# Attention of a hybrid encoder block: head pairs on 64-row tiles, first steps inside the last projection pair

## The chip, the core and the metric

The kernel is one program on one of the eight cores of a Trainium2 chip. A core has TensorE (PE, matrix products, with PEld for its weight loads), VectorE (DVE), ScalarE (ACT), GpSimd (POOL) and SyncE (SP, which only issues transfers); each works through its own queue in order. On-chip memory is SBUF (128 partitions) and PSUM (8 banks of 128 x 512 float32, where products land). The metric is device time in microseconds (us), smaller is better.

## The reference, cut to what matters

One layer on 1024 tokens of width 1024 in float32. After an RMS norm one projection gives all inputs of two branches:

```python
q, k, v, f_logit, g_b, g_c, hc, gate_conv, gate_attn = split(h @ w_in)
ya = g_b * causal_depthwise_conv(g_c * hc, conv_w)          # branch A, 512 channels
logf = log_sigmoid(f_logit + b_f); c = cumsum(logf)         # per head
logits = q @ k.T / 8 + c[t] - c[s], for s <= t only         # 8 heads of width 64
yb = softmax(logits) @ v                                    # branch B, 512 channels
merged = sigmoid(gate_conv) * (ya @ w_branch[0]) + sigmoid(gate_attn) * (yb @ w_branch[1])
x = x + rmsnorm(merged @ w_out)
x = x + rmsnorm(swiglu(rmsnorm(x)))                         # hidden width 2816
```

## The kernel before, in words

Products are made to nearly float32 accuracy from two reduced-precision parts. `split` rounds a matrix to `hi` on ACT (`copy`, L95) and takes the rest `lo` on DVE (`sub`, L89); `mm3` (L106 to L108) adds the three products hi hi, hi lo and lo hi. Large products are made by a Strassen-Winograd scheme (`strassen`), seven half-size products (`prod`) for a pair of 128-column weight blocks, whose sums are taken on DVE (`add`, L86).

The stages in order: norm and V projection; then `jobs`, 18 pairs of projections (4 of Q and K, 6 for the convolution, 8 pairs of the two gates), whose results go to DRAM (`qk_dram`, `ya_dram`, `sg_dram`, the last after a sigmoid); attention; branch B and the merge; the output product; the feed-forward part. Before the gate pairs are over, nothing of attention but the loads and splits of Q and K for the first pair can start: the PSUM pool `pss` opens only when the projections' pool `psm` of 8 banks closes.

Attention works through 64 units: 4 head pairs j, 8 blocks i of 128 query tokens (from the last to the first), 2 heads e. For a unit, `qk` (L708, L709) makes the logits of (i+1) x 128 keys. The 128 rows of the array hold a head's width of 64 twice: the stationary operand has q hi in one half and q lo in the other (`qk_stacks`), the moving operand k hi twice, then k lo twice, so two products per stretch of keys make all. Logits of over 512 keys take two banks (tile `sp`, tag S, two buffers of two banks). `softmax` adds the causal mask to the block of `cb` (c broadcast to all partitions) on POOL (L716), adds `cb` to the logits and takes the row minimum of the negated sum on DVE (L727), takes the exponential with its row sum on ACT (L731), and on DVE inverts the sum (L735) and scales the row (L736). `transp` turns the weights by 128 x 128 blocks on PE (L748) into the tile `tps` (two banks) and evacuates each four blocks on ACT (L95) or, one time in six, on DVE (L753). `pv_pair` (L764) multiplies with V, two heads on the two column halves of the array, and copies four query blocks at a time to `yb` on ACT.

Between units the products of branch A (`branch_a`, weights by `load_wa`, its product tile `pba`, one bank) fill PE; six of the eight row blocks of 128 output channels are made there, two (`RES`) after it. Each result is multiplied by its gate into `um` on DVE (L92). Then branch B splits its weights (`wbh`, `wbl`) and `yb` (`ybh`, `ybl`) and makes its products `pbb`.

The order of instructions on each engine is made when the program is built: a planner takes the instructions in program order, but lets one go ahead that its own estimate finds ready earlier. `tc.keep_in_program_order(ins)` pins an instruction behind the instruction traced before it on the same engine. Memory of a closed pool is used again, and the new tile waits for the readers of the tiles that it covers: `ybh` covers `yah`, which branch A reads to its end.

## Time and profile before

| what | us |
|---|---|
| median of 3 runs (1394.82 to 1399.31) | 1396.46 |
| the profiled execution | 1395.57 |
| its span, from the first to the last instruction | 1393.5 |
| TensorE busy | 1350.9 |
| VectorE, ScalarE, GpSimd busy | 967.1, 550.9, 141.1 |

The span is what the trace shows; the profiled execution has 2.1 us around it. The granted TensorE clock is 0.993 of full speed on average. In the rows below an instruction is named by its engine, its line, and `out<-in` by the program's tile names; a helper's line (L86, L89, L92, L95, L106 to L108) stands for all of its callers, so the tile names tell which one it is.

### The profile page before, as it was taken

The page shows a single profiled execution, that of the slowest core. Times are in us where ns is not written, and L with a number is a line of the kernel's source. Part 1 is how long each engine was busy: PE and PEld are TensorE (multiplying, and loading weights), DVE is VectorE, ACT ScalarE, POOL GpSimd, SP SyncE. Part 2 cuts the span into 40 slices and gives each one's busy share as a digit, 9 for nine tenths or more (in the row PEclk, how much of TensorE's full clock was granted, in tenths as well). Part 3 has the DMA queues.
Part 4 walks back from the last instruction along what each step waited for, and adds up shares of the span by engine and source line. Part 5 has one row for each costly group of instructions (what it writes and reads, how often), then busy time and mean ns, then how long its engine had stood idle before and what let it go on. Part 6 is the DMA issues. An engine that isn't in the chain of part 4 may idle for free.

```text
span 1393.5 us, 17697 instructions
## 1 busy us (share of the span) xinstructions
PE 1350.9 (97%) x6625; PEld 1108.1 (80%) x6625; DVE 967.1 (69%) x1557; ACT 550.9 (40%) x878; POOL 141.1 (10%) x260
## 2 busy tenths in 40 slices
PE   7999999999998999999999999999999999999987
PEld 6988888888886787778887788888888888888865
DVE  6883867655557787585669698776667766476695
ACT  6541222233347667433447332232232323444442
POOL 0001100011112222000001122100111101000000
PEclk9999999999999999999999999999999999999999
DMA  6332422333458432182234565222333326875471
GB/s 213 106 103 87 129 73 64 99 99 120 120 179 231 114 114 94 44 258 88 78 121 151 161 195 181 99 91 84 113 105 108 109 90 244 294 246 187 135 273 61
DMA packets 149670, 190.24 MB, mean 137 GB/s; under 512 B 9472, under 2 KB 102656, under 8 KB 149584
## 3 DMA queue, kind: packets, MB, share of 16 engines
q1 hardware_dynamic: 134272, 138.47, 32.8%
q0 software_dynamic: 15312, 50.64, 10.1%
q8 instruction: 52, 0.85, 0.3%
q14 instruction: 34, 0.28, 0.1%
HBM read 140.03 MB, written 49.05 MB: 136 GB/s over the span
## 4 chain that ended last, share of the span: by engine, by line
PE 88%; DVE 5%; DMA 3%; ACT 2%; issue 1%; SPq 0%; POOL 0%; DVEq 0%; ACTq 0%; POOLq 0%
PE b L106 18%; PE b L108 18%; PE b L107 18%; PE pd L106 4%; PE pd L108 4%; PE pd L107 4%; PE po L764 3%; PE tps L748 2%; PE pm L106 2%; PE pm L107 2%; PE pm L108 2%; PE pbb L107 1%; PE sp L708 1%; PE pbb L108 1%; DMA raw<-qk_dram 1%
## 5 line engine op out<-in xcount | busy, mean ns | idle before, releaser
L86 DVE TENSOR_TENSOR c<-c,b 128x512 f32<-128x512 f32 x200 | 136.5, 683 | 101.5 <-PE b L108 73.2
L95 ACT ACTIVATE hi<-raw 128x1024 fp32r<-128x1024 f32 x111 | 117.4, 1058 | 195.9 <-PE b L107 87.6
L89 DVE TENSOR_TENSOR lo<-raw,hi 128x1024 fp32r<-128x1024 f32 x104 | 127.1, 1222 | 97.5 <-PE b L108 69.0
L106 PE MATMUL b<-hth,hi 128*128 128x512 f32 x352 | 138.9, 395 | 0.0
L108 PE MATMUL b<-hth,lo 128*128 128x512 f32 x352 | 138.1, 392 | 0.0
L107 PE MATMUL b<-htl,hi 128*128 128x512 f32 x352 | 137.2, 390 | 0.0
L95 ACT ACTIVATE hi<-sx 128x1024 fp32r<-128x1024 f32 x40 | 42.5, 1061 | 221.3 <-PE b L107 195.7
L106 PE MATMUL pd<-hi 128*128 128x512 f32 x224 | 88.5, 395 | 5.1 <-DVE um L86 5.1
L108 PE MATMUL pd<-hi,lo 128*128 128x512 f32 x224 | 87.8, 393 | 0.0
L108 PEld LDWEIGHTS b<-hth,lo 128*128 128x128 f32 x352 | 66.1, 188 | 15.7
L107 PEld LDWEIGHTS b<-htl,hi 128*128 128x128 f32 x352 | 66.1, 188 | 14.7
L106 PEld LDWEIGHTS b<-hth,hi 128*128 128x128 f32 x352 | 66.2, 188 | 13.9
L89 DVE TENSOR_TENSOR lo<-sx,hi 128x1024 fp32r<-128x1024 f32 x40 | 49.0, 1225 | 34.4 <-PE b L108 30.8
L106 PE MATMUL b<-hah,hi 128*128 128x512 f32 x176 | 69.8, 399 | 1.5 <-ACT c L95 1.5
L89 DVE TENSOR_TENSOR sx<-raw 128x512 f32<-128x512 f32 x78 | 53.7, 688 | 22.5 <-DMA raw<-in_w_in_dram 12.2
L108 PE MATMUL b<-hah,lo 128*128 128x512 f32 x176 | 69.0, 393 | 0.0
L107 PE MATMUL b<-hal,hi 128*128 128x512 f32 x176 | 68.6, 390 | 0.0
L727 DVE CUSTOM_DVE_ANT_0 pt<-sp,cb 128x1024 f32<-128x1024 f32 (+7 forms) x64 | 48.1, 753 | 20.1 <-PE sp L709 9.8
L108 PE MATMUL b<-hT34h,lo 128*128 128x512 f32 x144 | 56.7, 394 | 0.0
L108 PE MATMUL b<-hT12h,lo 128*128 128x512 f32 x144 | 56.7, 394 | 0.0
L106 PE MATMUL b<-hT34h,hi 128*128 128x512 f32 x144 | 56.2, 390 | 0.4 <-DVE c L86 0.4
L731 ACT ACTIVATE pt<-pt,nm 128x1024 f32<-128x1024 f32 (+7 forms) x64 | 49.4, 772 | 17.9 <-DVE nm L727 15.9
(318 smaller groups left out, 3403.7 us busy)
## 6 DMA issues: line engine op xcount, KB each, us to landing
raw<-in_w_gate_up_dram SPq DMA_DIRECT2D x51, 512.0 KB, 4.0
raw<-in_w_in_dram SPq DMA_DIRECT2D x35, 512.0 KB, 4.2
graw<-in_w_down_dram SPq DMA_DIRECT2D x28, 512.0 KB, 5.0
a_dramS<-um POOLq DMA_DIRECT2D x44, 256.0 KB, 2.8
a_dramA<-um POOLq DMA_DIRECT2D x33, 256.0 KB, 2.9
xt<-in_x_dram SPq DMA_DIRECT2D x16, 512.0 KB, 4.2
raw<-qk_dram SPq DMA_DIRECT2D x32, 256.0 KB, 5.0
raw<-a_dramS SPq DMA_DIRECT2D x16, 512.0 KB, 3.7
```

The source lines that it names most:

```text
L86: nc.vector.tensor_tensor(o, a, b, op=ALU.add)
L89: nc.vector.tensor_tensor(o, a, b, op=ALU.subtract)
L95: nc.scalar.activation(o, a, AF.Copy)
L106: nc.tensor.matmul(ps, ah, bh, start=start, stop=False, **kw)
L107: nc.tensor.matmul(ps, ah, bl, start=False, stop=False, **kw)
L108: nc.tensor.matmul(ps, al, bh, start=False, stop=stop, **kw)
L708: nc.tensor.matmul(sp[:, b, :w], qs[:, qi], kh[:, k0:k1], start=True, stop=False)
L727: nc.vector.tensor_tensor_reduce(*args, 1.0, 3e38, op0=ALU.add, op1=ALU.min, accum_out=nm)
L731: nc.scalar.activation(pt[:, :n], pt[:, :n], AF.Exp, bias=nm, scale=-1.0, accum_out=rsum)
L748: nc.tensor.transpose(tps[:, k - k0, :], pt[:, k * P : (k + 1) * P], ident)
L764: nc.tensor.matmul(po[0][e * HD : (e + 1) * HD, i % 4, :], v[:, k, h * HD : (h + 1) * HD], pts[e][:, k, :], start=(k == 0), stop=(k == i),)
```

## The change

All of the following is one change.

- The last of the 18 projection pairs is written out by hand (`last_pair`) on two banks of its own (`pst`, tags ma and mb); the other pairs have 6 banks. Between its seven products stand the split of the first head pair's Q and K, the load of its V, and the logits and softmax of the first two steps. Its results are stored without the sigmoid, which is applied after they are loaded.
- A unit is now a step of both heads. Q and K of a pair are loaded once, with head 0 in partitions 0 to 63 and head 1 in 64 to 127, and the logits are products on 64 rows: q hi k hi, q hi k lo, q lo k hi, for head 0 and head 1 in turn, each head in its own bank.
- Row sums are kept; `inverse_rows` inverts them for a pair at once, turns them with a small transpose, writes them to DRAM and loads them broadcast, and `divide` scales `yb` with them instead of the weights.
- Order: every PE instruction of attention and of the last pair is pinned, and the splits of later operands on ACT and DVE. A step goes logits of t, softmax of t, first half of the transposes of t-1 (if it has more than four blocks), P.V of t-2, the other transposes; half a row block of branch A at the steps of `FILL`. The last pair takes query blocks 3 to 0 before 7 to 4, and its sums are inverted by halves.
- V is loaded per head pair by SP; `cb` has two buffers for even and two for odd pairs, `pt` likewise for steps; two of five evacuations of transposes go to DVE; gates are loaded by halves. In branch B `yb` is split ahead of the weights, the weights by halves.

```diff
-    def mm3(ps, a, b, start, stop, **kw):
+    def inorder(ins):
+        return tc.keep_in_program_order(ins)
+    def mm3(ps, a, b, start, stop, pin=lambda ins: ins, **kw):
...
-    psm, psm_close = pool("psm", 8, space=PSUM)
+    pst, pst_close = pool("pst", space=PSUM)
+    psm, psm_close = pool("psm", 6, space=PSUM)
...
+    def qk(j, i):
+        qh, ql, kh, kl = stacks[j]
...
+        for b, (k0, k1) in enumerate(parts):
+            for x, (q_, k_) in enumerate(((qh, kh), (qh, kl), (ql, kh))):
+                for e in range(2):
+                    r = slice(e * HD, (e + 1) * HD)
+                    out_ = sps[e][:, b] if wide else sps[0][:, e]
+                    inorder(
+                        nc.tensor.matmul(
+                            out_[:, : k1 - k0], q_[r, qi], k_[r, k0:k1],
+                            start=(x == 0), stop=(x == 2),
+                        )
+                    )
...
+    steps = [(j, i) for j in range(3) for i in reversed(range(ST))]
+    steps += [(3, i) for i in (3, 2, 1, 0, 7, 6, 5, 4)]
...
+    def last_pair(w):
...
+        pr(ma, "A11", B11, True)
+        copy(c21, ma)
+        inorder(nc.scalar.activation(warm, ones[:, 0:1], AF.Exp))
+        pr(mb, "A12", B21, True)
+        add(c11, c21, mb)
+        qk_split(0)
+        load_v(0)
+        pr(ma, "S2", T2, True)
+        add(c12, c21, ma)
+        pr(mb, "S1", T1, True)
+        add(c22, c21, mb)
+        step_qk(0)
+        pr(ma, "S3", T3, False)
+        add(c22, c22, ma)
+        step_softmax(0)
+        pr(mb, "S4", B22, False)
+        add(c12, c12, mb)
+        step_qk(1)
+        pr(ma, "A22", T4, False)
+        add(c21, c21, ma)
...
-        split(wh, wl, wr)
-        sg = tp_.tile([P, S], F32, tag="sg", name="sg", bufs=2)
-        nc.sync.dma_start(sg, sg_dram[d][0])
+        split(wh, wl, wr, inorder)
...
+    def inverse_rows(j, half=None):
...
+        nc.vector.reciprocal(ri, rs)
+        tr = pss.tile([P, 4, P], F32, tag="T", name="tr", bufs=2)[: 2 * w, 0, :]
+        inorder(nc.tensor.transpose(tr, ri.rearrange("p e i -> p (e i)"), ident))
...
+        nc.vector.tensor_copy(rT, tr)
+        for e in range(2):
+            nc.sync.dma_start(ri_dram[j][e][to]..., rT[e * w : (e + 1) * w, :])
...
+            nc.sync.dma_start(rb[e * HD : (e + 1) * HD, :], ri_dram[j][e][to].partition_broadcast(HD))
...
-        ri = st_tile("ri")
-        nc.vector.reciprocal(ri, rsum)
-        nc.vector.tensor_scalar(pt[:, :n], pt[:, :n], ri, None, op0=ALU.mult)
...
+    FILL = (7, 10, 13, 14, 15, 18, 21, 22, 23, 25, 26, 27)
+    step_softmax(1)
+    for t in range(1, NU + 4):
+        j, i = steps[t] if t < NU else (None, None)
+        if t > 2 and t < NU:
+            step_qk(t)
+            step_softmax(t)
+        if j is not None and j < 3 and i == 5:
+            cb_of(j + 1, 0)
+            cb_of(j + 1, 1)
+            qk_load(j + 1)
+            load_v(j + 1)
...
+            turn_ = transp(k_, pts.pop(t - 1), ptTs[t - 1])
+            if k_ > 3:
+                next(turn_)
+                next(turn_)
+            if t == 1:
+                step_qk(2)
+                step_softmax(2)
+        if 2 <= t < NU + 2:
+            pv_pair(*steps[t - 2], ptTs.pop(t - 2))
+        if t in FILL and steps[t - 1][1] < 4:
+            next(fill)
+        for _ in turn_:
+            pass
+        if t in FILL and steps[t - 1][1] > 3:
+            next(fill)
+        if j is not None and j < 3 and i == 4:
+            qk_split(j + 1)
+        if 2 <= t < 6:
+            load_ya(t - 2)
+        if t <= NU:
+            jj, ii = steps[t - 1]
+            if jj < 3 and ii == 0:
+                rbs[t + 3] = jj, inverse_rows(jj)
+            elif jj == 3 and ii % 4 == 0:
+                rbs[t + 3] = jj, inverse_rows(jj, ii // 4), ii // 4
+        if t in rbs:
+            divide(*rbs.pop(t))
...
     for d in range(KT - RES, KT):
         for _ in branch_a(d, load_wa(d), psm, "mm"):
             pass
...
-    for n in range(2):
-        ns = slice(n * NC, (n + 1) * NC)
+    for ns in (n1, n2):
         for k in range(4):
             split(ybh[:, k, ns], ybl[:, k, ns], yb[:, k, ns])
+        for k in range(4):
+            split(wbh[k][:, ns], wbl[k][:, ns], wbr[k][:, ns])
```

## The prediction

> **What bounds the kernel now.** I read the page first, then the busy time by stage, then the chain of waits and the timelines of the stages that lose time.

> ```profile
> span 1393.5 us, 17697 instructions
> PE 1350.9 (97%) x6625; PEld 1108.1 (80%) x6625; DVE 967.1 (69%) x1557; ACT 550.9 (40%) x878; POOL 141.1 (10%) x260
> ```

> TensorE is busy nearly throughout, so only idle or badly packed TensorE time can be won. The stages around attention (columns: time, then busy time and instructions of PE, weight loads, DVE, ACT and POOL, the granted clock, the DMA share, GB/s):

> ```profile
> 395.72:414.95 19.23, 19.23 (x86) 15.78 (x85) 9.89 (x11) 8.70 (x11) 2.30 (x5) 1.00 0.59 175
> 414.95:470.00 55.05, 46.74 (x324) 34.21 (x323) 41.50 (x90) 37.06 (x71) 14.51 (x23) 1.00 0.76 211
> 470.00:578.22 108.22, 106.61 (x879) 86.83 (x879) 83.73 (x218) 75.42 (x171) 26.35 (x45) 1.00 0.27 87
> 578.22:589.25 11.03, 11.03 (x49) 8.93 (x48) 2.06 (x3) 0.60 (x1) 0.00 (x0) 1.00 0.06 24
> 589.25:598.64 9.39, 6.71 (x21) 4.96 (x21) 9.19 (x12) 6.21 (x10) 0.00 (x0) 0.82 0.78 245
> ```

> The first row is the last projection pair. Attention runs from 414.95 to 578.22, 163.3 us; 578.22 to 589.25 is the two row blocks of branch A that are left over (48 products of 512 columns, 0.23 us each); 589.25 to 598.64 is the start of branch B, with PE idle and the clock at 0.82. In its first 55 us attention finishes 324 PE instructions, in the next 108 us 879. The chain of waits shows two long transfers in that first part, and the waits of PE what else holds it:

> ```profile
> 422.47 14.52 DMA raw<-qk_dram
> 460.13 7.79 DMA cb<-c_dram
> ```

> ```profile
> PE sp L708 <- DVE nm L727: 4.8, 3, 2.2
> ```

> Unit prices, from chain and timeline rows:

> ```profile
> 474.68 0.87 PE tps L748 x8
> 477.03 1.89 PE po L764 x30
> ```

> ```profile
> 476.10 0.93 PE L748 MATMUL tps<-ident,pt 128*128 128x128 f32 x7
> 476.96 1.96 PE L764 MATMUL po<-ptT,v 128*64 128x128 f32 x30
> 478.85 0.98 PE L748 MATMUL tps<-ident,pt 128*128 128x128 f32 x7
> 485.00 0.40 PE L108 MATMUL pba<-yah,s4l 128*128 128x512 f32 x1
> 485.23 0.40 PE L708 MATMUL sp<-lo,hi 128*128 128x512 f32 x1
> ```

> A transpose takes 0.87/8 = 0.109 us. A P.V product on a half-width tile takes 1.89/30 = 0.063 us; two of these, on the two column halves, take the 0.109 us of one full-width instruction, plus the entry and exit of the burst: after seven transposes (0.76 us) the next starts 0.86 later, so a change of tile shape costs 0.1 us. A 512-column logits product follows the one before by 0.23 us, which is 0.446 ns per column.

> The instruction counts of the whole stage, and below them those of the part after 470 for lines 708, 709, 748 and 764:

> ```profile
> L764 PE MATMUL po<-ptT,v 128*64 128x128 f32 x576 | 44.9, 280 | 2.2 <-DMA v<-v_dram 1.4 <-DVE ptT L753 0.4 <-ACT ptT L95 0.2
> L748 PE MATMUL tps<-ident,pt 128*128 128x128 f32 x288 | 43.1, 276 | 2.4 <-ACT ptT L95 1.6 <-DVE pt L736 0.5 <-ACT pt L731 0.2
> L736 DVE TENSOR_SCALAR pt<-pt,ri 128x1024 f32<-128x1024 f32 (+7 forms) x64 | 35.9, 561 | 1.2
> L735 DVE RECIPROCAL ri<-rsum 128x1 f32<-128x1 f32 x64 | 10.1, 158 | 9.3 <-ACT pt L731 8.8
> L92 DVE TENSOR_TENSOR um<-sg,pba 128x512 f32<-128x512 f32 x12 | 8.2, 682 | 2.0 <-PE pba L108 1.9
> ```

> ```profile
> 470.00:578.22 108.22, 23.91 (x66) 12.29 (x66) 1.00 0.27 87
> 470.00:578.22 108.22, 22.60 (x66) 12.43 (x66) 1.00 0.27 87
> 470.00:578.22 108.22, 32.00 (x216) 25.10 (x216) 1.00 0.27 87
> 470.00:578.22 108.22, 32.24 (x432) 24.56 (x432) 1.00 0.27 87
> ```

> Before, logits stream 4 x 4608 columns per pair, 73,728 in all: 32.8 us. 288 transposes: 31.4. 576 P.V products: 36.3. 144 branch products (six row blocks): 33.1. Sum 133.6 us of the 163.3. For the part after 470: logits 132/192 of 32.8 = 22.6, transposes 216 = 23.5, P.V 432 = 27.2, the other 99 instructions 22.8: 96.1 us took 108.2, a factor of 1.126. The first 55 us did the other 37.5, a factor of 1.47. So the stage loses about 17.5 us to its start and 12 us to its running.

> **The change part by part.**

> *Logits on 64-row tiles.* Today both heads stream 2 products of n columns on all rows; afterwards a head needs 3 products on its 64 rows, and the heads alternate. If the two row halves run together, a pair costs 3n instead of 4n columns: 24.6 us, 8.2 less. If they take turns it costs 6n: 49.2 us. No row of this trace has a 64-row tile. The nearest is the P.V product on column halves, where two cost the time of one; I take 24.6 and keep 49.2. [...]

> *Tile shape changes.* A step with more than four key blocks goes logits, transposes, P.V, transposes: two changes more than the P.V price holds; a smaller one goes logits, P.V, transposes: one more. 16 x 2 + 16 x 1 = 48 changes at 0.1 us: 4.8 us.

> *Normalisation.* The 64 scalings (L736) and 64 reciprocals (L735), 35.9 and 10.1 us of DVE, leave the chain softmax to transpose. In their place come five reciprocals and small transposes (5 x 0.109 = 0.5 us of PE), a trip of the inverse sums through DRAM, and eight 512-column products at the price of L92, 5.5 us of DVE. DVE is no bound here (83.73 of 108.22), so this shortens waits rather than the sum. Two of five evacuations go to DVE instead of one of six, 22 more at up to 0.69: it gives back 15 us of what it won.

> *PE sum after.* 24.6 + 31.4 + 36.3 + 33.1 + 4.8 + 0.5 = 130.7 us, including the two first logits that move into the last projection pair (about 3 us of it, which lengthen the 19.23 us there; PE has no gap there that could hide them).

> *Order by hand.* Every PE instruction of the stage is pinned in program order, so PE waits for the one that is late. I compare engines step by step:

> ```profile
> L727 DVE CUSTOM_DVE_ANT_0 pt<-sp,cb 128x1024 f32<-128x1024 f32 x8 | 9.8, 1220 | 6.1 <-POOL cb L716 6.0
> L731 ACT ACTIVATE pt<-pt,nm 128x1024 f32<-128x1024 f32 x8 | 9.2, 1153 | 7.6 <-DVE nm L727 7.5
> L727 DVE CUSTOM_DVE_ANT_0 pt<-sp,cb 128x640 f32<-128x640 f32 x8 | 6.6, 822 | 3.3 <-PE sp L709 3.3
> L95 ACT ACTIVATE ptT<-tps 128x512 f32<-128x512 f32 x44 | 25.2, 593 | 15.1 <-PE tps L748 14.9
> L753 DVE COPY ptT<-tps 128x512 f32<-128x512 f32 x4 | 2.7, 686 | 0.4 <-PE tps L748 0.4
> L89 DVE TENSOR_TENSOR yal<-raw,yah 128x1024 fp32r<-128x1024 f32 x3 | 3.5, 1218 | 0.0
> L625 ACT ACTIVATE hi<-raw 128x1024 fp32r<-128x1024 f32 x4 | 4.2, 1049 | 1.6 <-DMA raw<-qk_dram 1.6
> ```

> A step of eight blocks needs DVE 2 x 1.22 + 1.6 evacuations of 0.69 = 3.5 us, ACT 2 x 1.15 + 2.4 x 0.59 = 3.7, against PE 1.4 logits + 1.7 transposes + 2.0 P.V + 0.2 = 5.3. At the first step of a pair the P.V and transposes of the small last blocks are all that PE has beside the logits (1.4 + 0.7 + 0.3 = 2.4), and DVE's 2.44 gates the next logits, since a wide step takes both S buffers: about 1 us, three times. At five blocks with the split of the next pair, DVE has 2 x 0.82 + 0.8 + 2 x 1.22 = 4.9 and ACT 2.1 extra, against PE 4.1: about 1 us, three times; steps 2 to 5 carry load_ya too (ACT 1.05, DVE 1.22 each), another 2 us. These are the waits that come next; half of them I count in the running factor. So 130.7 x 1.126 = 147.2, plus 2: 149.2. Ends: a factor of 1.06 (half of today's loss), 138.5, and today's mean over both parts, 1.22, 159.5; up to 1.27 as a rival below.

> *What the start loses today* goes: first logits, exponentials and the table load sit under four products of 2.7 us each, whose DVE and ACT are half idle (9.89 and 8.70 of 19.23). Q and K are loaded once instead of twice per head, V per pair by SP instead of 2 MB at once by POOL, and the masked sums get their own buffers for odd pairs, so the 14.52 and 7.79 us transfers are no longer what PE waits for: they are issued two steps (about 8 us) before their split, against 4.4 to 7.8 us of landing. POOL keeps the mask additions alone. The psum pool of the projections goes from 8 banks to 6: free, since a job holds three and 0.68 us additions empty them under the next job.

> *The tail.* Today 578.22 to 598.64 is 20.4 us: 11.03, then 9.39, of which 21 products are 4.8.

> ```profile
> 590.18 2.11 PE L106 MATMUL pbb<-ybh,hi 128*128 128x512 f32 x8 [0.77 <-ACT ybh L95]
> 594.20 0.50 PE L107 MATMUL pbb<-ybl,hi 128*128 128x512 f32 x1 [1.91 <-DVE ybl L89]
> 597.67 0.63 PE L106 MATMUL pbb<-ybh,hi 128*128 128x512 f32 x1
> 598.10 0.47 PE L107 MATMUL pbb<-ybl,hi 128*128 128x512 f32 x1
> 590.05 3.49 DVE L89 TENSOR_TENSOR wbl<-raw,hi 128x1024 fp32r<-128x1024 f32 x3
> ```

> PE starts 0.77 late, has only first products until 594.20 (ybl stands behind three wbl in DVE's queue), then runs at half speed (0.43 between starts) until 598.1. Afterwards yb is split ahead of the weights, in halves, and the weights can be split earlier: 1.3 us lost there (0.77 and one subtraction) instead of 4.6. But load_wa for the left-over blocks pins its DVE subtraction behind the last division of yb, which waits for the inverse sums' way out and back:

> ```profile
> c_dram<-cT POOLq DMA_DIRECT2D x1, 32.0 KB, 3.0
> cb<-c_dram SPq DMA_DIRECT2D x8, 512.0 KB, 4.4
> ```

> From the last small transpose: copy 0.3, out 3.0, back 4.4 (a larger transfer), division 0.68, subtraction 0.69: 9.1 us. PE meanwhile has the last P.V (1.3), waits for the copy of po and the rounding of wa (1.2), then four products (0.9): it stands still for about 5 us, and the clock row above prices the restart at 1.6. The second block's subtraction is pinned behind the last um product: 1.0. Sum: 11.0 + 1.2 + 5 + 1.6 + 1.0 + 1.3 + 4.8 = 25.9, 5.5 more than today; ends 0 wait (19.3, -1.1) and 7 (+7.5). The four late sigmoids and their table load fall where ACT has 0.60 us in 11.03: nothing.

> *Sum.* 1395.57 (the profiled execution; 1393.5 span plus 2.1 around it; the median of the runs is 0.9 above) - 163.3 + 149.2 + 5.5 = 1387.0.

> **The rivals.** (1) *Little is lost, and the round trip is hidden:* factor 1.06 and no wait in the tail: 1395.6 - 24.8 - 1.1 = 1370. For it: the normalisation left the chain, and no long transfer is waited for. Against: the hand order cannot give way.
> (2) *The row halves take turns:* logits 49.2, PE sum 155.3; DVE and ACT are then covered, so 1.06: 164.6. With the tail: 1395.6 + 1.3 + 5.5 = 1402, slower. It decides once over half of a product stays uncovered: 0.56 x (164.6 - 149.2) eats the 8.6 us. Against it: the P.V pairs.
> (3) *The hand order stalls every step:* PE waits for DVE at the S buffers (2.2 us the longest such wait today) about 1 us a step: factor 1.27, 166: 1404, slower.
> (4) *A change of shape empties the array:* a transpose lasts 276 ns in its group row and starts every 109, so a full emptying would cost up to 0.28 instead of 0.1. 48 x 0.18 = 8.6 us more: 1396, no change. [...]

> **How the numbers follow.** The forecast has 0.47; (1) 0.17; (2) 0.13; (3) 0.09; (4) and other ends within 0.3% 0.14. What a measurement can tell from no change is 0.3%, 4.2 us. Faster 0.64, same 0.14, slower 0.22. The forecast's own range is 1379 to 1391; with (1), and (2) up to its price, 1368 to 1403.

> **What would show it.** In the changed profile: of each two logits products of 64 rows the second starts within some 10 ns of the first and the third 0.23 later at 512 columns (right), or each 0.23 later (rival 2). PE's first idle time after the last projection product under 2 us. Attention, from the last projection product to the last P.V, near 146 us. In the tail a PE wait of about 5 us ended by DVE s4l, with a division behind a load of ri_dram ahead of it in DVE's queue; if that is absent the tail is 5 us shorter. Waits of sp for nm at each pair's first steps. What makes me wrong: pairs that take turns, PE waits at most steps, or late landings of qk_dram at the split, which hold ACT and DVE at the pin.

## The result: slower, and the profile after

The changed kernel takes 1416.68 us (median; 1414.39 to 1421.78) against 1395.64 us for the kernel before (1394.26 to 1399.31) on the same chip: a ratio of 1.0146, 95% interval 1.0123 to 1.0169. The profiled execution took 1416.07 us. The forecast was 1387.0 within 1368 to 1403: wrong in sign, and outside its range by 13.7 us.

The head of the page of the changed kernel:

```profile
span 1414.3 us, 17729 instructions
...
PE 1354.4 (96%) x6726; PEld 1104.8 (78%) x6726; DVE 938.9 (66%) x1467; ACT 537.1 (38%) x855; POOL 132.2 (9%) x256
```

TensorE's busy time grew by 3.5 us only and VectorE's fell by 28; of the 20.8 us by which the span grew, TensorE was idle in 17.3 (59.9 us of the span against 42.6). The stages (columns as in the prediction: time, busy time and instructions of PE, weight loads, DVE, ACT, POOL, granted clock, DMA share, GB/s):

```profile
397.12:419.80 22.68, 22.68 (x110) 17.67 (x109) 9.82 (x13) 7.23 (x10) 3.12 (x6) 1.00 0.74 242
419.80:453.79 33.99, 27.24 (x248) 21.62 (x246) 21.61 (x45) 22.86 (x48) 8.73 (x15) 0.85 0.28 97
453.79:480.00 26.21, 21.96 (x157) 16.55 (x158) 13.26 (x25) 10.46 (x21) 4.03 (x8) 0.87 0.40 130
480.00:560.00 80.00, 75.19 (x620) 57.88 (x619) 44.72 (x106) 44.06 (x105) 15.35 (x32) 1.00 0.39 116
560.00:596.60 36.60, 27.83 (x259) 21.38 (x256) 16.05 (x36) 20.22 (x41) 2.75 (x6) 0.91 0.07 23
596.60:615.36 18.76, 13.52 (x50) 9.95 (x49) 4.58 (x8) 4.35 (x7) 0.00 (x0) 0.91 0.15 43
615.36:659.80 44.44, 44.12 (x193) 35.88 (x193) 38.26 (x56) 14.26 (x19) 0.00 (x0) 1.00 0.69 225
```

The last projection pair grew from 19.23 to 22.68 us, since two steps' logits now lie in it. Attention, the four rows behind it, takes 176.8 us against 163.3. Its PE idle time (the difference of the two first columns) is 6.75 + 4.25 + 4.81 + 8.77 = 24.6 us, and the clock column shows 0.85, 0.87 and 0.91 in the three stretches that hold most of it. The two left-over row blocks take 18.76 us against 11.96, branch B 44.44 against 47.47 (before, 590.18 to 637.65). What PE waits for, from the view of the waits (total, times, longest):

```profile
PE tr L807 <- ACT ptT L95: 10.9, 3, 6.5
...
PE tps L832 <- DVE ptT L838: 4.6, 3, 2.6
...
PE pba L111 <- DVE s4l L89: 3.3, 2, 2.9
...
PE sp L598 <- DVE nm L620: 2.8, 3, 1.6
```

The first two are for evacuations of transposed tiles (`ptT`), which the prediction did not have among the waits. Four places on PE's timeline hold most of the lost time (in square brackets the idle time ahead and what ended it):

```profile
442.77 0.47 PE L832 MATMUL tps<-ident,pt 128*128 128x128 f32 x1 [2.64 <-DVE ptT L838]
...
464.25 0.38 PE L807 MATMUL tr<-ident,ri 128*16 128x128 f32 x1 [4.16 <-ACT ptT L95]
...
574.42 0.38 PE L807 MATMUL tr<-ident,ri 128*8 128x128 f32 x1 [6.49 <-ACT ptT L95]
...
601.88 0.71 PE L111 MATMUL pba<-yah,s4l 128*128 128x512 f32 x1 [2.87 <-DVE s4l L89]
```

What stood in the way at each of them, from the timelines of ACT and DVE. At 574, on ACT:

```profile
568.60 1.28 ACT L772 ACT_TABLE_LOAD   x1 [3.00 <-DMA sg<-sg_dram]
569.90 0.63 ACT L772 ACTIVATE sg<-sg 128x512 f32<-128x512 f32 x1
570.54 1.28 ACT L624 ACT_TABLE_LOAD   x1
571.84 1.15 ACT L624 ACTIVATE pt<-pt,nm 128x1024 f32<-128x1024 f32 x1
...
574.12 0.42 ACT L95 ACTIVATE ptT<-tps 128x128 f32<-128x128 f32 x2
```

ACT holds the deferred sigmoid of the last gate, which waits 3.00 us for its load; two table loads of 1.28 us stand around it; behind it stand two exponentials (the first is shown), and only behind those the evacuation of a transposed tile, whose buffer the small transpose `tr` needs. PE's order is pinned, so it does nothing for 6.49 us. At 464 the pinned rounding of a branch A weight stands in the same place on ACT, and its subtraction on DVE; the exponential behind them waits for DVE's softmax:

```profile
460.20 0.63 ACT L95 ACTIVATE s4h<-s 128x512 fp32r<-128x512 f32 x1 [2.24 <-DMA s<-in_w_branch_dram]
462.79 1.15 ACT L624 ACTIVATE pt<-pt,nm 128x1024 f32<-128x1024 f32 x1 [1.96 <-DVE nm L620]
...
463.94 0.26 ACT L95 ACTIVATE ptT<-tps 128x128 f32<-128x128 f32 x1
```

```profile
460.86 0.69 DVE L89 TENSOR_TENSOR s4l<-s,s4h 128x512 fp32r<-128x512 f32 x1 [2.70 <-ACT s4h L95]
461.47 1.22 DVE L620 CUSTOM_DVE_ANT_0 pt<-sp,cb 128x1024 f32<-128x1024 f32 x1
```

The load of `s` landed at 460.2, the pinned subtraction stands ahead of the softmax (L620), so the exponential and the evacuation behind it are late. Run 2 shows how much of the 4.16 us is due to this pin. At 442 it is the split of the next pair's Q and K and a `load_ya`, three subtractions in a row ahead of the softmax of a step and of an evacuation:

```profile
437.40 1.23 DVE L566 SCALAR_TENSOR_TENSOR lo<-raw,hi 128x1024 fp32r<-128x1024 f32 x1 [1.45 <-ACT hi L563]
438.54 1.22 DVE L89 TENSOR_TENSOR kl<-kl,hi 128x1024 fp32r<-128x1024 f32 x1
439.68 1.22 DVE L89 TENSOR_TENSOR yal<-raw,yah 128x1024 fp32r<-128x1024 f32 x1
440.81 0.68 DVE L620 CUSTOM_DVE_ANT_0 pt<-sp,cb 128x512 f32<-128x512 f32 x1
...
442.03 0.68 DVE L838 COPY ptT<-tps 128x512 f32<-128x512 f32 x1
```

At 601 it is the tail's round trip, as the prediction had it: the division waits for the inverse sums and the subtraction of the weights is pinned behind it.

```profile
600.53 0.69 DVE L92 TENSOR_TENSOR yb<-yb,rb 128x512 f32<-128x512 f32 x1 [4.90 <-DMA rb<-ri_dram]
601.14 0.69 DVE L89 TENSOR_TENSOR s4l<-s,s4h 128x512 fp32r<-128x512 f32 x1
```

Around each of these the granted clock is halved for one or two stretches of 3.41 us, two of the five places here:

```profile
441.62:448.44 6.82, 5.67 (x35) 4.57 (x35) 3.57 (x9) 4.69 (x11) 2.70 (x4) 0.50 0.35 120
...
571.32:578.14 6.82, 3.71 (x17) 2.77 (x18) 0.94 (x2) 3.20 (x7) 0.00 (x0) 0.50 0.04 15
```

At half clock products of 512 columns start 0.43 us apart (602.40 and 602.83), with the clock whole again 0.23 (606.34 and 606.57). All five places between 397 and 660 last 27.3 us, of which PE is busy 20.85: by these distances about half of it, 10.4 us of work, is lost, 8.7 of it in attention. So attention lost about 24.6 + 8.7 = 33.3 of its 176.8 us; by this estimate it would have taken 143.5 without both, close to what was forecast.

### The profile page after: what moved, and what is told of

Same layout as the page of the kernel before. It is cut to its first block, busy times and chain, and to the rows that moved or that the text cites. A ratio compares the mean times of both kernels' runs of the same rounds, so it can differ in the third digit from the quotient of the medians.

```text
span 1414.3 us, 17729 instructions
## 1 busy us (share of the span) xinstructions
PE 1354.4 (96%) x6726; PEld 1104.8 (78%) x6726; DVE 938.9 (66%) x1467; ACT 537.1 (38%) x855; POOL 132.2 (9%) x256
## 4 chain that ended last, share of the span: by engine, by line
PE 81%; DVE 8%; DMA 4%; ACT 3%; issue 3%; POOL 0%; DVEq 0%; SPq 0%; ACTq 0%; POOLq 0%
PE b L109 16%; PE b L111 16%; PE b L110 16%; PE pd L109 5%; PE pd L111 5%; PE pd L110 5%; PE po L851 2%; PE sp L598 2%; PE tps L832 2%; PE pm L111 2%; PE pm L109 2%; PE pm L110 2%; PE pba L109 1%; PE pba L111 1%; PE pba L110 1%
## 5 line engine op out<-in xcount | busy, mean ns | idle before, releaser
L86 DVE TENSOR_TENSOR c<-c,b 128x512 f32<-128x512 f32 x195 | 133.2, 683 | 93.4 <-PE b L111 68.6
L89 DVE TENSOR_TENSOR lo<-raw,hi 128x1024 fp32r<-128x1024 f32 x104 | 127.1, 1222 | 98.3 <-PE b L111 69.4
L95 ACT ACTIVATE hi<-raw 128x1024 fp32r<-128x1024 f32 (+1 forms) x111 | 114.6, 1034 | 189.3 <-PE b L110 75.9
L95 ACT ACTIVATE hi<-sx 128x1024 fp32r<-128x1024 f32 (+1 forms) x42 | 43.7, 1040 | 222.8 <-PE b L110 198.0
L109 PEld LDWEIGHTS b<-hth,hi 128*128 128x128 f32 x352 | 66.1, 188 | 14.9 <-DVE c L86 1.1
L89 DVE TENSOR_TENSOR lo<-sx,hi 128x1024 fp32r<-128x1024 f32 x40 | 49.0, 1225 | 34.4 <-PE b L111 30.8
L89 DVE TENSOR_TENSOR sx<-raw 128x512 f32<-128x512 f32 x78 | 53.7, 689 | 23.7 <-DMA raw<-in_w_in_dram 11.5
L620 DVE CUSTOM_DVE_ANT_0 pt<-sp,cb 128x1024 f32<-128x1024 f32 (+7 forms) x64 | 46.2, 755 | 20.8 <-PE sp L598 17.5
L624 ACT ACTIVATE pt<-pt,nm 128x1024 f32<-128x1024 f32 (+7 forms) x64 | 49.1, 769 | 23.0 <-DVE nm L620 22.8
L832 PE MATMUL tps<-ident,pt 128*128 128x128 f32 x288 | 46.3, 298 | 8.7 <-DVE ptT L838 4.6
L111 PE MATMUL b<-hT34h,lo 128*128 128x512 f32 x136 | 53.4, 393 | 0.0
L111 PE MATMUL b<-hT12h,lo 128*128 128x512 f32 x136 | 53.4, 393 | 0.0
## 6 DMA issues: line engine op xcount, KB each, us to landing
raw<-in_w_gate_up_dram SPq DMA_DIRECT2D x51, 512.0 KB, 3.9
raw<-in_w_in_dram SPq DMA_DIRECT2D x35, 512.0 KB, 4.0
graw<-in_w_down_dram SPq DMA_DIRECT2D x28, 512.0 KB, 5.0
xt<-in_x_dram SPq DMA_DIRECT2D x16, 512.0 KB, 4.5
raw<-a_dramS SPq DMA_DIRECT2D x16, 512.0 KB, 3.6
raw<-a_dramA SPq DMA_DIRECT2D x15, 512.0 KB, 5.0
```

The costliest lines, as they stand in the source:

```text
L86: nc.vector.tensor_tensor(o, a, b, op=ALU.add)
L89: return nc.vector.tensor_tensor(o, a, b, op=ALU.subtract)
L95: return nc.scalar.activation(o, a, AF.Copy)
L109: pin(nc.tensor.matmul(ps, ah, bh, start=start, stop=False, **kw))
L111: pin(nc.tensor.matmul(ps, al, bh, start=False, stop=stop, **kw))
L620: nc.vector.tensor_tensor_reduce(*args, 1.0, 3e38, op0=ALU.add, op1=ALU.min, accum_out=nm)
```

## The experiments

All kernels are edits of the changed kernel. The theory: a few operands come late, and the halved clock adds to the price. The rivals: the hand-written order of PE stalls it everywhere; the row halves of the 64-row products take turns. The results first; "first pm" is the start of the first output product in the trace, which leaves out the part behind it: from there to the end of the span the fourteen kernels take 752.1 to 757.0 us, though no edit touches that part, so some 2 us of a whole time either way are not explained here. Runs 1 to 4, 5 to 8 and 9 to 12 were taken on three chips, with the kernel before at 1397.0, 1396.6 and 1396.8 us; each ratio is to the kernel before on its own chip, and differences in us to the change carry up to 1.4 us of that.

| run | time, us | ratio to before, 95% interval | first pm, us |
|---|---|---|---|
| before | 1395.64 | 1 | 637.65 |
| the change | 1416.68 | 1.0146 (1.0123 to 1.0169) | 659.80 |
| 1 sigmoids last | 1408.16 | 1.0083 (1.0056 to 1.0110) | 653.59 |
| 2 load_wa unpinned | 1406.32 | 1.0073 (1.0050 to 1.0096) | 651.50 |
| 3 all splits unpinned | 1408.55 | 1.0095 (1.0067 to 1.0122) | 654.42 |
| 4 load_wa(6) early | 1410.14 | 1.0101 (1.0074 to 1.0127) | 652.68 |
| 5 heads not alternating | 1418.08 | 1.0156 (1.0138 to 1.0174) | 661.81 |
| 6 PE order free | 1404.63 | 1.0059 (1.0040 to 1.0077) | 648.87 |
| 7 sigmoids last, load_wa unpinned | 1401.15 | 1.0029 (1.0018 to 1.0041) | 645.63 |
| 8 as 7, split at three blocks | 1395.91 | 0.9994 (0.9984 to 1.0005) | 639.90 |
| 9 as 7, PE order free | 1391.38 | 0.9962 (0.9949 to 0.9974) | 634.15 |
| 10 as 8, later small transpose | 1400.21 | 1.0026 (1.0014 to 1.0037) | 641.75 |
| 11 as 7, sigmoids as before | 1401.65 | 1.0037 (1.0025 to 1.0049) | 647.77 |
| 12 as 8, PE order free | 1388.83 | 0.9944 (0.9930 to 0.9958) | 632.58 |

### 1. The last gate's sigmoids behind the last rounding

```diff
-                nc.scalar.activation(sg, sg, AF.Sigmoid)
+                inorder(nc.scalar.activation(sg, sg, AF.Sigmoid))
```

> Edit: the last gate's sigmoids at the load of branch A are pinned in program order, so that ACT applies both behind the rounding of the last row block instead of ahead of the exponentials of step (3,7). Theory 'few late operands': the 6.49 us gap of PE before the small transpose at 574.42 goes, and with it the 6.8 us at half clock from 571.3 (at most 3.4 us of work), while the tail takes one more 0.63 us sigmoid: about 9 us less than the changed kernel, 1407, ratio to before near 1.008. Rival 'hand order': the pinned PE finds the next late operand, ACT's evacuation behind two exponentials of 1.15 us: a gap of 3 us or more stays there and the time falls by 3 us or less, 1413 or more. Rival 'new place, same wait': the sigmoids and the table load hold the tail instead: its 18.8 us grow by 2 to 4 us and the gain is 5 to 7 us.

Measured: 1408.16 us, 8.5 less than the change. The gap of 6.49 us is gone; the longest wait of `tr` for ACT is now the one at 462, 3.57 us:

```profile
PE tr L807 <- ACT ptT L95: 4.1, 3, 3.6
```

From the last P.V to the first `pbb` it is 19.9 us instead of 19.0, so the tail took 0.9 of it back, not 2 to 4. The first theory holds. Up to the first output product the gain is 6.2 us. Nothing in the changed kernel made the planner put the sigmoid late.

### 2. The rounding of branch A's weights unpinned

```diff
-        split(wh, wl, wr, inorder)
+        split(wh, wl, wr)
```

> Edit: the rounding and the subtraction of load_wa lose their pin, so that the planner places them. Theory 'few late operands': the 4.16 us gap at 464.25 with its 6.8 us at half clock (3.4 us of work), and in the tail the 2.87 us gap at 601.88 with 3.4 us at half clock (1.7) go: 12 us less than the changed kernel, 1405, ratio near 1.006. Rival 'hand order of PE': the gaps turn up at neighbouring steps; 1413 or more. Rival 'the round trip': only the gap at 464 goes, the tail still waits for the inverse sums; 1409.

Measured: 1406.32 us, 10.4 less than the change, against 12 expected. Of the 8.3 us up to the first output product, 5.9 are the tail (last P.V to first `pbb` 13.1 us instead of 19.0), because the planner now brings the weights of the left-over blocks into attention, ahead of the last division. The gap at 464 shrank from 4.16 to 1.86 us and did not go: `tr` still finds the evacuation behind an exponential of 1024 columns. So of the 4.16 us the pin on the weight made about 2.3, and the last P.V comes 2.2 us earlier (594.12 instead of 596.33). The gap at 574 stayed (6.69 us), as it has another cause.

### 3. All splits unpinned

```diff
-        split(wh, wl, wr, inorder)
+        split(wh, wl, wr)
-        split(yah[:, m, :], yal[:, m, :], yr, inorder)
+        split(yah[:, m, :], yal[:, m, :], yr)
-        late = inorder if j else lambda ins: ins
+        late = lambda ins: ins
```

> Edit: as the run before, and load_ya and the split of Q and K of the later pairs lose their pins too; only PE's order stays written by hand. Theory 'few late operands': beside the 12 us of the run before, the 2.64 us gap at 442.77 and its 6.8 us at half clock (3.4) go: 18 us less than the changed kernel, 1399, ratio near 1.002. Rival 'hand order of PE': 1410 or more. Rival 'a free split comes too late or too early': a split of Q and K that the planner puts ahead of an exponential or behind a step's softmax makes a new PE wait of 2 us or more at a pair's start, and the time is no better than the run before.

Measured: 1408.55 us, no better than the run before (2.2 us more, with intervals that overlap). The last rival is right in kind: a split that the planner put too early makes a new wait. It is not one of Q and K but the rounding of the first two blocks of `load_ya`, ahead of the exponentials of step 1 in ACT's queue. On ACT's timeline

```profile
428.21 1.06 ACT L95 ACTIVATE yah<-sx 128x1024 fp32r<-128x1024 f32 x1 [6.81 <-DMA kl<-qk_dram]
...
430.12 1.03 ACT L624 ACTIVATE pt<-pt,nm 128x896 f32<-128x896 f32 x1
```

The exponentials stand behind a wait of 6.81 us, which by the profile a load ended (it names that of `kl`, which is not this instruction's operand; which transfer it needed is not settled). On PE:

```profile
435.63 0.69 PE L832 MATMUL tps<-ident,pt 128*128 128x128 f32 x2 [8.39 <-ACT ptT L95]
```

The profiled execution is the longest of this kernel's four, 1413.20 us against 1407.50 to 1408.79, so part of this wait may belong to it alone. That some of these pins pay is suggested, not shown; and the run does not tell those of `load_ya` from those of Q and K.

### 4. The tail alone

```diff
-            nxt = load_wa(d + 1) if d + 1 < KT - RES else None
+            nxt = load_wa(d + 1)
```

with the last operands of the filler handed to the first left-over block.

> Edit: the weights of the first left-over row block are loaded and split with the last block inside attention, ahead of the last division. Theory: the waits of 1.20 and 2.87 us at the first left-over block go with their 3.4 us at half clock (1.7): 5 us less than the changed kernel, 1412, ratio near 1.011; the row blocks then run while the inverse sums travel. Rival 'branch B needs the division anyway': the first pbb product waits for the rounding of yb, which follows the same division, and 2 us or less are won: 1415.

Measured: 1410.14 us, 6.5 less. Last P.V to first `pbb`: 13.8 us instead of 19.0. The tail's wait was real: its removal shortens the tail by 5.2 us, near the 5 expected, and branch B did not wait for the division instead (PE's longest wait for `ybh` stays 0.7 us).

### 5. Heads not alternating

```diff
-            for x, (q_, k_) in enumerate(((qh, kh), (qh, kl), (ql, kh))):
-                for e in range(2):
+            for e in range(2):
+                for x, (q_, k_) in enumerate(((qh, kh), (qh, kl), (ql, kh))):
```

> Edit: in every block of logits the three products of one head are issued ahead of the three of the other, instead of alternating; nothing else changes. Theory 'the row halves run together': in the changed kernel a pair of 64-row products costs one (0.23 us at 512 columns); in this order only the seams between the heads can overlap, 9 instead of 6 units in a step of two blocks and 5 instead of 3 in a step of one, so logits of 24.6 us become 38, 13 us more; some of it falls into waits that are there anyway: 8 to 13 us above the changed kernel, 1425 to 1430. With no overlap at the seams: up to 24.6 more, 1441. Rival 'the halves take turns already': no change, 1417.

Measured: 1418.08 us; the ratio's interval covers that of the change. By the number written above this would be the rival's result; the timeline says why it is not. In the changed kernel each two products start together (column x2), the second two 0.34 us after the first, which follow a product of another shape, and the third 0.23 us later:

```profile
408.20 0.50 PE L598 MATMUL sp<-hi 64*128 64x512 f32 x2
408.54 0.39 PE L598 MATMUL sp<-kl,hi 64*128 64x512 f32 x2
408.77 0.39 PE L598 MATMUL sp<-hi,lo 64*128 64x512 f32 x2
...
409.47 0.39 PE L598 MATMUL sp<-hi,lo 64*128 64x512 f32 x2
409.79 0.50 PE L109 MATMUL ma<-hT34h,hi 128*128 128x512 f32 x1
```

In run 5 head 0's three products are issued ahead of head 1's three, and yet:

```profile
407.78 0.51 PE L598 MATMUL sp<-hi 64*128 64x512 f32 x2
408.12 0.40 PE L598 MATMUL sp<-kl,hi 64*128 64x512 f32 x2
408.36 0.40 PE L598 MATMUL sp<-hi,lo 64*128 64x512 f32 x2
```

The first products of the two heads start within 10 ns, although in the program's order two products of head 0 stand between them. So over these three products a row half worked through its own and did not wait for the other half's: in 0.58 us, from 407.78 to 408.36, three pairs started. So the edit does not undo the pairing, and the experiment cannot price it; but it shows that the pairing needs no strict alternation. What the new form of the logits gains is in their busy time over attention (time, then busy time and instructions of PE on `sp`, granted clock, DMA share, GB/s), in the kernel before

```profile
414.95:578.22 163.27, 48.72 (x192) 1.00 0.44 129
```

and in run 8, where the clock is nearly whole:

```profile
419.76:581.70 161.94, 33.24 (x264) 0.98 0.38 121
```

48.72 us became 33.24. For the change of tile shape the changed kernel's rows show about 0.1 us: 0.32 us from the last pair at 409.47 to the next full-width product at 409.79, instead of 0.23.

### 6. PE's order left to the planner

```diff
-                    inorder(
-                        nc.tensor.matmul(
-                            out_[:, : k1 - k0], q_[r, qi], k_[r, k0:k1],
+                    free(
+                        nc.tensor.matmul(
+                            out_[:, : k1 - k0], q_[r, qi], k_[r, k0:k1],
```

and likewise, with `free` returning its argument, for the transposes, the small transposes, P.V and the row blocks.

> Edit: the PE instructions of attention (logits, transposes, small transposes, P.V, row blocks of branch A) lose their pins; the planner orders PE, as in the kernel before. The pins of load_wa, load_ya and the splits of Q and K and those of the last projection pair stay. Rival 'hand order of PE' is right if the time falls by more than 10 us below the changed kernel (under 1407). Theory 'few late operands' says that the planner, which does not see the late transfers, only shuffles the same waits: the time stays within 8 us of the changed kernel (1409 to 1425), and PE's gaps longer than 0.15 us between 397 and 625 still sum to 20 us or more (29.6 in the changed kernel).

Measured: 1404.63 us, 12.1 less: the rival's bound (under 1407) is met, and PE's gaps over 0.15 us sum to 10.8 us, not 20 or more. My theory, that a planner without sight of the late transfers only shuffles the waits, falls; that PE now has other work ahead of the waiting instruction fits this. The deferred sigmoid stands where it stood, yet `tr` waits only 0.9 us for its evacuation. The free order has a price: the logits' busy time in attention is 41.23 us (34.73 in the changed kernel, by the same view),

```profile
420.19:584.60 164.41, 41.23 (x264) 0.99 0.33 102
```

because the two heads of some steps then run one behind the other: 76 of the 264 products start without a partner, 4 in the changed kernel. Here six products of one head stand ahead of the other's six, and a product alone takes as long as a pair does (0.2 us from start to start at 448 columns; the pairs of the changed kernel at 415.81 and 416.01 as well):

```profile
558.46 0.47 PE L601 MATMUL sp<-hi 64*128 64x448 f32 x1 [0.37 <-DVE nm L623]
558.77 0.36 PE L601 MATMUL sp<-kl,hi 64*128 64x448 f32 x1
558.98 0.36 PE L601 MATMUL sp<-hi,lo 64*128 64x448 f32 x1
...
559.58 0.35 PE L601 MATMUL sp<-hi,lo 64*128 64x448 f32 x1
559.61 0.47 PE L601 MATMUL sp<-hi 64*128 64x448 f32 x1
```

### 7. The first two together

The sigmoids are queued behind the last copy of `po`:

```diff
-        split(wh, wl, wr, inorder)
+        split(wh, wl, wr)
-                nc.scalar.activation(sg, sg, AF.Sigmoid)
+                with tc.issue_after(po[1].ins):
+                    nc.scalar.activation(sg, sg, AF.Sigmoid)
```

> Edit: load_wa unpinned as in the second run, and the last gate's two sigmoids queued behind the last copy of po. Theory 'few late operands': the two savings are of different places and add up: 8.5 + 10.4 = 19 us below the changed kernel, 1397, ratio near 1.001; PE's gap ahead of the small transpose of the last pair (6.49 us at 574) is under 1 us. Rival 'one cause seen twice' (the gap at 574 gives the waits of the tail their length): 10 to 12 us below, 1405.

Measured: 1401.15 us, 15.5 less than the change, against 19. Up to the first output product the savings add up: 6.2 (run 1) and 8.3 (run 2) against 14.2. They are separate places. PE's gap ahead of the last small transpose fell from 6.49 to 0.32 us, as the theory had written.

### 8. The split of Q and K two steps later

```diff
-        if j is not None and j < 3 and i == 4:
+        if j is not None and j < 3 and i == 2:
             qk_split(j + 1)
```

on top of run 7.

> Edit: as the run before, and Q and K of the next pair are split at the step with three key blocks instead of the one with five. Theory: the waits of PE behind the two DVE subtractions of 1.22 us (0.78 + 2.64 us at 439 to 443 with 6.8 us at half clock, 0.75 at 487, 0.51 + 1.40 at 529) shrink to under 1 us a pair, since a step of three blocks leaves DVE and ACT more time under the row blocks: 5 us below the run before, 1392, ratio near 0.997: under the kernel before. Rival 'the subtractions only move': the first step of the next pair waits for them instead, gain under 1 us, 1396 to 1397.

Measured: 1395.91 us, 5.2 less than run 7: the 5 us expected, but 4 us above the 1392 written, since run 7 came 4 us above its own 1397. The kernel is now level with the one before the change. Under 1 us a pair holds for the second and the third split; at the first PE waits 1.91 us (448.51) for an evacuation that ACT makes behind the roundings moved there. Attention takes 161.94 us (176.8 in the changed kernel), 14.5 of it idle:

```profile
419.76:581.70 161.94, 147.44 (x1278) 113.77 (x1276) 95.33 (x209) 94.22 (x212) 32.46 (x61) 0.98 0.38 121
```

### 9. Both cures with PE's order free

Run 7's edit and run 6's.

> Edit: the seventh run (sigmoids behind the last copy of po, load_wa unpinned) with PE's order left to the planner as in the sixth. Run 6 fell 12 us below the changed kernel and run 7 15.5 us. Theory 'late operands cost time because PE's pinned order cannot give way': both undo the same waits inside attention, and only the tail's (about 5 us) is left to add: 5 us below run 6, 1399 to 1400, not better than run 7 by more than 2 us. Rival 'two separate losses': 12 + 15.5 = 27.5 us below, 1389, ratio 0.995.

Measured: 1391.38 us, 25.3 less than the change. My theory (the same waits, seen twice) is refuted, and the rival holds: 12.1 + 15.5 = 27.6 expected by it, and up to the first output product 10.9 + 14.2 = 25.1 against 25.7. Six of run 7's 14.2 us are the tail, which run 6 leaves as it is (20.1 us from the last P.V to the first `pbb`; 13.1 here). For the others the rows give only part of the reason: in run 6 more logits run without a partner than here (busy 41.23 us there, 38.71 here). The rest stays open.

### 10. Smaller waits

On top of run 8, the small transpose of a pair moves behind the next step's logits, and the evacuations given to DVE shift by one:

```diff
-                if evac_n[0] % 5 in (1, 3):
+                if evac_n[0] % 5 in (2, 4):
...
+        if t in late:
+            rbs[t + 2] = late[t][0], inverse_rows(*late[t]), *late[t][1:]
```

> Edit: run 8, with the small transpose one step later (behind the next step's logits; the one at the very end stays) and the evacuations to DVE shifted by one, so that ACT takes the first. Theory: the waits ahead of the small transpose (1.86, 0.66, 0.32 us in run 8) go, and the first wait of attention (1.61 + 0.60 us at 422) loses the 0.6 us copy that stands ahead of the softmax of step 1: 2 to 3 us below run 8, 1393, ratio near 0.998. Rival 'the wait moves to the next user of the transposed tile': no more than 1 us, 1395.

Measured: 1400.21 us, 4.3 more than run 8: a miss on the other side of both expectations. The waits of `tr` shrank from 3.4 to 0.6 us, others took their place:

```profile
PE sp L598 <- DVE nm L620: 5.6, 8, 1.9
...
PE po L852 <- DVE ptT L839: 3.3, 3, 2.6
```

The wait of logits for the softmax rose from 3.3 to 5.6 us, and a P.V product waits 2.65 us for an evacuation that now falls to DVE behind the three subtractions of a split. Up to the first output product the two traces differ by 1.9 us; the rest lies behind it, in the part that the edit does not touch (756.4 against 752.8 us in the traces), and is not explained.

### 11. Sigmoids as before the change

Run 7 with the sigmoids in the last projection job, ahead of the store, and none at the loads.

```diff
+            nc.scalar.activation(so, c11, AF.Sigmoid)
+            for t in (c12, c21, c22):
+                nc.scalar.activation(t, t, AF.Sigmoid)
             for r, c, t in ((0, n1, so), (0, n2, c12), (1, n1, c21), (1, n2, c22)):
                 nc.gpsimd.dma_start(sg_dram[j][r, :, c], t)
```

> Edit: run 7 with the last gate's sigmoids back in the last projection job, ahead of the store, as in the kernel before (none is applied at the loads). If deferring them saves what the start shows: four sigmoids of 0.63 us and two table loads of 1.28 us stand between the last projection product and the first exponentials: 3 to 5 us above run 7, 1405. Rival: they fall where ACT waits for the softmax anyway (1.6 us at the start): within 1.5 us of run 7.

Measured: 1401.65 us, the same as run 7 (the rival's case). So deferring the sigmoids won nothing that the whole time shows; in the changed kernel it cost 8.5 us (run 1) by where they landed.

### 12. Everything

Run 8 with PE's order free.

> Edit: run 8 with PE's order left to the planner (sigmoids behind the last copy of po, load_wa unpinned, split of Q and K at three key blocks). Theory as in run 9: with the late operands gone, a free PE order wins little beyond run 8: 1393 to 1396, ratio 0.997 to 1.000. Rival 'two separate losses': 1384 to 1387, ratio 0.992.

Measured: 1388.83 us, a ratio to the kernel before of 0.9944 (0.9930 to 0.9958): faster than both kernels. By the written numbers it lies between the theory (1393 to 1396) and the rival (1384 to 1387), nearer the rival: a free order is worth 7.1 us beyond run 8. Attention, the left-over blocks, branch B:

```profile
421.60:575.00 153.40, 150.13 (x1278) 115.20 (x1276) 95.15 (x209) 93.97 (x212) 30.45 (x61) 1.00 0.41 128
575.00:587.82 12.82, 11.41 (x50) 8.96 (x49) 3.00 (x5) 3.83 (x6) 0.00 (x0) 1.00 0.13 42
587.82:632.58 44.76, 44.09 (x192) 35.89 (x192) 38.60 (x56) 14.28 (x19) 0.00 (x0) 1.00 0.68 223
```

The clock is whole in all three, PE idles 3.3 us in attention, and 1388.83 lies 1.8 us above the forecast; that is no support for it, since this is another kernel than the one forecast.

## Why the prediction was wrong

By its own steps, on the profiled executions: 1416.07 - 1387.0 = 29.1 us. Attention holds 30.6 of it (176.8 against 149.2 less the 3 us counted to the last pair), the last pair and what lies before it 1.9; the tail came 1.7 better and the rest 1.7.

*Order by hand*, the step that failed. The prediction took a "running factor" of 1.126 from the part after 470 and counted half of the new waits into it, plus 2 us. Its own row shows that this factor had no room for waits: of 108.22 us there PE was busy 106.61, idle 1.61. The factor is how the work packs (what is in it the rows do not separate), and it came out right: the changed kernel's attention without idle time and half clock is about 143.5 us, against 147.2 less the 3 moved to the last pair, 144.2. The waits had to be counted on top, one by one: they were 24.6 us idle and 8.7 us lost at half clock, against 2. Even by its own words the prediction was short there: the waits that it named sum to 3 + 3 + 2 = 8 us, half of which is 4.

*The four late sigmoids: nothing.* Wrong, and the largest loss from a term put at nothing: run 1 gives 8.5 us, 6.2 of them up to the first output product. The sum asked whether ACT has room in the tail; it did not ask where in ACT's queue the sigmoid lands. It is not pinned, its load stood in the transfer queue, where SP spent 11.18 us on issuing three loads of gates, and it landed ahead of the exponentials of step (3,7) with two table loads.

```profile
554.85 11.18 SPq L770 DMA_DIRECT2D sg<-sg_dram  x3
```

*Splits in the way.* "About 1 us, three times" at five blocks: measured 0.78 + 2.64, 0.75, 0.51 + 1.40 us, with 6.8 us at half clock at the first; run 8 gives 5.2 us. The pinned rounding of `load_wa` was weighed in the tail alone; inside attention it made about 2.3 of the 4.16 us at 464, and its removal brought the last P.V 2.2 us forward (run 2).

*The clock.* The prediction priced a restart once, 1.6 us in the tail. In the changed kernel five places at half clock lie between 397 and 660.

*Logits on 64-row tiles*: right in mechanism and better in size. Pairs start together, 0.23 us apart at 512 columns, the distance of single full-width products (rival 2 refuted); 15.5 us less busy time in attention (48.72 to 33.24 in run 8, 34.73 in the changed kernel, partly at half clock), where 8.2 and the 3 moved to the last pair were forecast.

*Tile shape changes* at 0.1 us: right. Rival 4, a full emptying at 0.28 us, is refuted by the 0.32 us from 409.47 to 409.79.

*What the start loses* goes: right in the main (the waits for `qk_dram` and `cb` are gone), the first wait is 1.61 us and 0.60 behind it, 2.2 together, where under 2 was forecast. *Six banks are free*: off by 1.1 us; the first projections wait 1.80 us for ACT's copy of a bank (before 0.69).

*The tail*: right in sum. Forecast 5.5 us more in all, measured 63.20 against 59.43 from the last P.V to the first output product, 3.8 more; the wait for `s4l` behind the division was foreseen, but at about 5 us, and it is 2.87: from the small transpose to the end of the subtraction 6.8 us passed (595.05 to 601.83), where 9.1 had been added up. With the wait for `s4h` and the half clock, run 4 gives 5.2 us of the tail and 6.5 of the whole time for removing it.

*Rival 3* came nearest: PE waits because its order cannot give way. The mechanism it named was another (the S buffers: 2.8 us of waits in all, not a microsecond a step) and its 1404 us 12.7 too low. Run 6 puts the pins on PE at 12.1 us, run 8 the late operands at 20.8; together, in run 12, they are worth 27.9, so about 5 us are counted in both.

## What to carry to other kernels

When an engine's order is pinned, list for every pinned instruction the one it waits for and what stands ahead of that in its queue; a factor taken from a stage whose engine was busy all the time holds no waits. An instruction that is moved "to where there is room" needs its place in the queue secured, above all on ACT, where one sigmoid between exponentials cost two table loads of 1.28 us around it (568.60 and 570.54 in the changed kernel). And before pinning an order by hand, try which pins pay: here those on PE and on `load_wa` did not (runs 6 and 2), and whether those on the other splits did, run 3 leaves open.

## What the runs showed of the hardware

Products on different row halves of the array ran side by side even with three of one half ahead of the other's in PE's queue (run 5: the two first start together at 407.78, the next two at 408.12). With six ahead, as in run 6, the other half's first started at 559.61, 1.15 us behind the first of the six (558.46) and 0.03 behind the last (559.58). So in run 5 PE's products did not start strictly in the order of its queue, though the opening lets every engine work in order.
